# Low-half products one slab later, squares summed on TensorE and scalings on VectorE at the changes of sub-layer

## The chip, the core and the metric

The kernel runs on one core of one Trainium2 chip. The metric is the device time of one execution in microseconds, from the first to the last instruction with what lies around them; the lower the better. The core's engines work side by side, each through its own queue in order: PE (TensorE) multiplies matrices, with the weight loads shown apart as PEld; DVE (VectorE) and POOL (GpSimd) do elementwise work; ACT (ScalarE) copies, casts and applies functions; SP issues most DMAs. Semaphores join the queues.

## What is computed

A decoder trunk of two layers over 512 positions of width 1024. Each layer has four sub-layers: a half-step SwiGLU feed-forward (here "ffn1"), token mixing by three head groups with one output projection ("mix"), a second half-step feed-forward ("ffn2"), and a gated per-layer embedding ("ple"). Every sub-layer stands between two RMS norms and is added to the residual:

```python
for i in range(DEPTH):
    h = rmsnorm(x, g_ffn1_pre[i])
    x = x + 0.5 * rmsnorm(swiglu(h, w1_gate[i], w1_up[i], w1_down[i]), g_ffn1_post[i])
    h = rmsnorm(x, g_mix_pre[i])
    ...
    x = x + rmsnorm(mixed, g_mix_post[i])
    h = rmsnorm(x, g_ffn2_pre[i])
    x = x + 0.5 * rmsnorm(swiglu(h, w2_gate[i], w2_up[i], w2_down[i]), g_ffn2_post[i])
    h = rmsnorm(x, g_ple_pre[i])
    e = jax.nn.sigmoid(h @ w_ple_gate[i]) * (p[i].astype(x.dtype) @ w_ple_proj[i])
    x = x + rmsnorm(e, g_ple_post[i])
```

So between two sub-layers the program must finish the post-norm of the one, add to the residual x, and square, sum and scale x for the pre-norm of the next. This happens seven times (three times in a layer, and once between the layers); they are called **changes** below. After the last sub-layer there is only the post-norm and the output.

## The kernel before

x lies transposed in the core's memory: eight tiles (K slabs) of 128 features by 512 positions, in fp32. Every product is made of three matmuls in a rounded fp32 form: the weight and the input are each split into a high half and a low remainder (`wh`, `wl`, `xh`, `xl`), and the matmuls are wh·xh, wh·xl and wl·xh. They stand in `product` (lines 285, 286 and 287 in this order), so each weight tile of 128 columns takes 3 × 8 matmuls for the eight K slabs.

A change runs through two pieces of code, in two halves of 256 positions (`HALVES`, a and b).

`finish` (line 512) ends a sub-layer. It makes the last output tiles half by half; the outputs y are squared on ACT, and where a sub-layer makes more than two tiles in halves (mix: eight) the squares are added up ("folded", line 443) on POOL. Sums of squares over the features are matmuls of a square tile against a column of ones (`Rstd.add`, line 388; the tile `st`): a square tile is the loaded weight, and one column moves. In the program each is one matmul for 128 positions; in the profile each shows as two MATMUL rows. Nine small DVE steps turn `st` into the reciprocal root `rt` (line 368). PE transposes it (line 401, tile `rb`) and ACT copies the broadcast row out (`rbs`, line 402). Then `update` does the residual for each slab k: `scale` (line 570) multiplies y by the row, on DVE for even k and on POOL for odd k, and `add` (line 573) multiplies by the gain, a column, and adds x, on DVE.

`Entry` (line 449) begins the next sub-layer while `update` runs. For each slab ACT writes xh = x·gain (line 466), DVE writes xl = x·gain − xh (line 469), and ACT squares x; POOL folds the eight squares into one tile (line 443). The DVE queue in it is written by hand: update(k+1) stands ahead of xl(k). `products` (line 477) has PE's order by hand for half a: for each slab k, the three products of each of the `FIRST` = 3 first weight tiles; after slab `ROW_AT` = 5 it puts `row_b`, the transposes for half b of the row above. Then half b is updated, split and multiplied in the same way, with a fourth tile of whole width and, in ple, other work beside it. Behind the last of these products come the `st` matmuls over the squares of x, the nine small steps, and the row for the pre-norm, which the evacuations of the first tiles need.

All else (the order of most instructions within an engine's queue) is chosen by a scheduler when the program is built; SP's queue is the same before and after. In the four feed-forwards the gain is a column `half`, half of the post gain; the down-projection's outputs are copied from PSUM to y by DVE (lines 830 and 843), and the last tile's square is made from y (line 524).

Of the kernel before, what the change touches and what calls it, by code (L numbers as in the profile page):

```python
# [14 lines left out]
AF = mybir.ActivationFunctionType  # L15
ALU = mybir.AluOpType
# [6 lines left out]
NK = D // P  # L23
# [7 lines left out]
AT_DOWN = (3, 13)  # L31
# [4 lines left out]
FIRST = 3  # L36
ROW_AT = 5
MORE = 1
PROJ = 8
LAST_POOL = (2, 6)  # L40
DIRECT = 2
# [66 lines left out]
HALVES = (slice(0, S // 2), slice(S // 2, S))  # L108
# [49 lines left out]
def hybrid_trunk(ctx: ExitStack, tc: tile.TileContext, a: dict, out: bass.AP):  # L158
    nc = tc.nc
    V, A, T, G = nc.vector, nc.scalar, nc.tensor, nc.gpsimd  # L160
# [7 lines left out]
    def slot(dt=F32, name="s", tag="s"):  # L168
        return sp.tile([P, S], dt, tag=tag, name=name, bufs=SLOTS[tag])
# [35 lines left out]
    x = [cst.tile([P, S], F32, name=f"x{k}") for k in range(NK)]  # L205
# [26 lines left out]
    half = cst.tile([P, DEPTH, 2, 8], F32, name="half")  # L232
    for l in range(DEPTH):
        for i, n in enumerate(("ffn1_post", "ffn2_post")):
            V.tensor_scalar(out=half[:, l, i, :], in0=gains[:, l, G_COLS[n]:G_COLS[n] + 8],
                            scalar1=0.5, scalar2=None, op0=ALU.mult)
# [41 lines left out]
    def product(o, w, xs, first=True, cols=slice(0, S), tick=lambda: None, last=True):  # L278

        oc = o[:, cols]  # L280
        n = len(xs)
        for k in range(n):
            (wh, wl), (xh, xl) = w[k], xs[k]
            kw = dict(skip_group_check=True)
            T.matmul(oc, wh, xh[:, cols], start=first and k == 0, stop=False, **kw)  # L285
            T.matmul(oc, wh, xl[:, cols], start=False, stop=False, **kw)  # L286
            product.last = T.matmul(oc, wl, xh[:, cols], start=False, stop=last and k == n - 1, **kw)  # L287
            tick()
# [160 lines left out]
    class Entry:  # L449
# [3 lines left out]
        def __init__(self, l, name, update, row_b, tag):  # L453
            self.l, self.name, self.update, self.row_b = l, name, update, row_b
            self.xs = [(slot(F32R, "xh", tag), slot(F32R, "xl", tag)) for _ in range(NK)]
            self.tiles = [slot(name="sq") for _ in range(4)]
            self.sqs = [self.half(HALVES[0])]

        def half(self, c):
            sq = Squares(c, tiles=self.tiles)  # L460
            with tc.manual_schedule(engines={V.engine}):
                self.update(0, c)
                for k in range(NK):
                    g = gain(self.l, self.name, k)
                    h, lo = (t[:, c] for t in self.xs[k])
                    ia = A.activation(out=h, in_=x[k][:, c], func=AF.Copy, scale=g)
                    if k + 1 < NK:
                        self.update(k + 1, c)
                    iv = V.scalar_tensor_tensor(out=lo, in0=x[k][:, c], scalar=g, in1=f(h), op0=ALU.mult,  # L469
                                                op1=ALU.subtract)  # L470
                    sq.add(x[k][:, c])
            sq.fold()
            if c is HALVES[0]:
                self.tail = ia.ins, iv.ins
            return sq

        def products(self, tiles, more=lambda: None):


            ca, cb = HALVES  # L480
            with tc.manual_schedule(engines={T.engine}):
                for k in range(NK):
                    for w, o in tiles:
                        product(o, w[k:k + 1], self.xs[k:k + 1], k == 0, ca, last=k == NK - 1)
                    if k == ROW_AT:
                        self.row_b()
            self.sqs.append(self.half(cb))
            for w, o in tiles:
                product(o, w, self.xs, False, cb)
            more()  # L490
            self.eps = eps_col()
            r = Rstd(D, keep=self.eps)
            with tc.issue_after(product.last.ins):
                for sq, c in zip(self.sqs, HALVES):
                    r.add(*sq.parts(), cols=c, last=True)
            self.rt = r.col()
            self.r, self.behind = r, rsqrt_cols.last.ins

# [13 lines left out]
    def finish(ys, sq, last, compute, evac, gcol, nxt, at, xtag="s", eps=None):  # L512


        rb = slot(name="rbs")
        row_tag = "d" if nxt and nxt[1].startswith("ffn") else None
        direct = {m: slot(name="sq") for m in list(last)[-DIRECT:]}
        tiles = [slot(name="sq") for _ in range(3 if len(last) > DIRECT else 0)]

        def evacuate(m, c, o, sqh, parts):  # L520
            if m in direct:
                t = direct[m]
                evac(m, c, o)
                A.activation(out=t[:, c], in_=ys[m][:, c], func=AF.Square)
                parts.append(t)
            else:
                evac(m, c, o)
                sqh.add(ys[m][:, c])

        ca, cb = HALVES  # L530
        ra, rb_ = Rstd(D, ca, eps=eps), Rstd(D, cb, eps=eps)
        sqa, sqb = (Squares(c, tiles=tiles) for c in HALVES)
        pa, pb, steps = [], [], [0]
        sq.fold()
        for m in last:
            evacuate(m, ca, compute(m, ca), sqa, pa)
            if len(pa) == 1:
                sqa.fold()

        def tick():  # L540
            steps[0] += 1
            if steps[0] == at[0]:
                ra.add(*sq.parts(), *sqa.parts(), *pa, last=True)
                ra.col()
            elif steps[0] == at[1]:
                ra.row(rb[:, ca], None)
                rb_.add(*sq.parts())

        with tc.manual_schedule(engines={T.engine}):
            for m in last:  # L550
                o = compute(m, cb, tick)
                rb_.add(*pb[-1:])
                evacuate(m, cb, o, sqb, pb)
                if len(pb) == 1:
                    sqb.fold()
            assert steps[0] >= at[1]
            rb_.add(*sqb.parts())
        rb_.add(*pb[-1:], last=True)

        def row_b():  # L560
            rb_.row(rb[:, cb], row_tag)

        def update(k, c):
            scale(k, c)
            add(k, c)

        def scale(k, c):
            y = ys[k][:, c]
            e = G if k % 2 or nxt is None and k in LAST_POOL else V
            e.tensor_tensor(out=y, in0=y, in1=rb[:, c], op=ALU.mult)  # L570

        def add(k, c):
            V.scalar_tensor_tensor(out=x[k][:, c], in0=ys[k][:, c], scalar=gcol(k), in1=x[k][:, c],  # L573
                                   op0=ALU.mult, op1=ALU.add)
            if nxt is None:
                nc.sync.dma_start(out=out[:, k, c], in_=x[k][:, c])

        if nxt is None:
            with tc.manual_schedule(engines={V.engine}):
                order = [k for k in range(NK) if k % 2 == 0 and k not in LAST_POOL]  # L580
                order += [k for k in range(NK) if k not in order]
                for k in order:
                    scale(k, ca)
                todo = list(order)

                def between():
                    if todo:
                        add(todo.pop(0), ca)

                between()  # L590
                between()
                rb_.col(between)
                while todo:
                    between()
                row_b()
                for k in order:
                    update(k, cb)
            return None
        rb_.col()
        return Entry(*nxt, update, row_b, xtag)  # L600
# [119 lines left out]
    def ffn(l, idx, state, nxt, xtag="s", early=None):  # L720
# [85 lines left out]
        sq, ys = Squares(), {}  # L806
# [13 lines left out]
        for m in range(NK - LAST_DOWN):  # L820
            if early is not None and m == TRIG_AT:
                early()
            if m < TOGETHER:
                o = together[m]
            else:
                o = bank()
                product(o, down(m), hid)
            ys[m] = slot(name="y")
            sq.add(o)
            V.tensor_copy(out=ys[m], in_=o)  # L830
        last = range(NK - LAST_DOWN, NK)
        w = {m: down(m) for m in last}

# [6 lines left out]
            ys[m] = slot(name="y")  # L840

        def evac(m, c, o):
            V.tensor_copy(out=ys[m][:, c], in_=o[:, c])

        return finish(ys, sq, last, compute, evac, lambda k: half[:, l, idx, k:k + 1], nxt, AT_DOWN, eps=state.eps)

    def trig():

# [481 lines left out]
    state = start()  # L1330
    for l in range(DEPTH):
        state = ffn(l, 0, state, (l, "mix_pre"), xtag="m" if l else "s", early=None if l else trig)
        state = mixer(l, state, (l, "ffn2_pre"))
        state = ffn(l, 1, state, (l, "ple_pre"))
# [59 lines left out]
```

## Time and profile before

Three runs took 2153.1, 2151.86 and 2143.6 us; the median is 2151.86.

| | us |
|---|---|
| median of the runs | 2151.86 |
| profiled execution, its own time | 2149.54 |
| its span, first to last instruction | 2147.7 |
| POOL folds of squares (line 443), 165 of them, busy | 174.1 |
| POOL scalings (line 570), 68 of them, busy | 60.3 |

A row of the profile's timeline has the start in us, the duration, engine, line, operation and the tile written `<-` the tiles read; behind it in brackets stands how long the engine was idle before, and what released it. A row of windows gives, for a stretch of time, the busy time of each engine with the count of its instructions, the granted TensorE clock (PEclk, 1.00 is full speed), and the DMA share and rate. The seven changes lie at about 355, 612, 990, 1060, 1425, 1685 and 2055 us of the span.

### The profile page before, as it was taken

Reading aid. Unit: us, or ns where it says so; the run is one execution under the profiler, and the core shown is the slowest. Engines: PE = TensorE matmul, PEld = TensorE weight load, DVE = VectorE, ACT = ScalarE, POOL = GpSimd, SP = SyncE. Lnnn points to the kernel's source line nnn. Section 1 sums busy time; section 2 is a strip of 40 time slices with the busy share of each in tenths; the row PEclk is TensorE's granted clock in tenths of the full one; section 3 lists DMA queues with packets and bytes.
Section 4 is the critical chain, followed back from the end, with each engine's and each line's share of the span. In section 5 each row is a group of like instructions: output and inputs, shape, how many; then the busy total and the mean of one; then the engine's idle time right before and its main releaser. Section 6 shows DMA issues by size and latency. Waiting matters only on the chain.

```text
span 2147.7 us, 35941 instructions
## 1 busy us (share of the span) xinstructions
PE 2066.4 (96%) x13264; PEld 1879.5 (88%) x13264; DVE 1552.6 (72%) x2851; ACT 1117.2 (52%) x2296; POOL 507.4 (24%) x498
## 2 busy tenths in 40 slices
PE   7999999999999999999889999999999999999996
PEld 6999988887888999888779999888878889998886
DVE  7788754878879888625798886357788798885376
ACT  6556533555656555524565555235555565564243
POOL 3111012226432111003431110131264421100043
PEclk9999999999999999999999999999999999999998
DMA  7667232211233776332427762323111348653321
GB/s 218 171 175 180 86 109 72 88 62 47 59 80 107 187 179 152 99 96 82 123 84 189 175 169 86 103 67 99 53 52 54 81 133 191 181 136 97 98 74 65
DMA packets 139425, 244.73 MB, mean 114 GB/s; under 512 B 15600, under 2 KB 26096, under 8 KB 139248
## 3 DMA queue, kind: packets, MB, share of 16 engines
q1 hardware_dynamic: 117792, 204.00, 30.1%
q0 software_dynamic: 20736, 37.76, 11.0%
q8 instruction: 104, 1.70, 0.3%
q10 hardware_dynamic: 720, 0.67, 0.1%
q14 instruction: 73, 0.60, 0.1%
HBM read 240.27 MB, written 2.10 MB: 113 GB/s over the span
## 4 chain that ended last, share of the span: by engine, by line
PE 81%; DVE 13%; ACT 2%; issue 2%; DMA 1%; POOL 0%; SPq 0%; DVEq 0%; ACTq 0%; POOLq 0%
PE ps L286 9%; PE ps L285 9%; PE ps L287 9%; PE ux L686 6%; PE ux L685 6%; PE ux L684 6%; PE uy L686 3%; PE uy L685 3%; PE uy L684 3%; DVE x L573 2%; PE in L286 2%; PE in L287 2%; PE in L285 2%; DVE wl L270 2%; DVE xl L469 2%; PE uz L686 2%
## 5 line engine op out<-in xcount | busy, mean ns | idle before, releaser
L270 DVE TENSOR_TENSOR wl<-raw,wh 128x512 fp32r<-128x512 f32 (+2 forms) x893 | 603.9, 691 | 393.7 <-ACT wh L269 342.2
L269 ACT CAST wh<-raw 128x512 fp32r<-128x512 f32 (+1 forms) x934 | 548.6, 605 | 578.1 <-PE ps L286 269.4
L443 POOL TENSOR_TENSOR sq<-sq 128x256 f32<-128x256 f32 (+1 forms) x165 | 174.1, 1056 | 734.8 <-ACT sq L433 730.6
L286 PE MATMUL ps<-l,wh 128*128 128x512 f32 (+1 forms) x824 | 302.8, 367 | 0.2 <-DVE l L198 0.2
L287 PE MATMUL ps<-h,wl 128*128 128x512 f32 (+1 forms) x824 | 301.9, 367 | 0.0
L285 PE MATMUL ps<-h,wh 128*128 128x512 f32 (+1 forms) x824 | 300.5, 368 | 0.0
L668 POOL DMA_DIRECT2D raw<-in_w_gu x144 | 125.9, 912 | 676.6 <-DMA raw<-in_w_gu 227.5
L686 PE MATMUL ux<-fh,wl 128*128 128x256 f32 x864 | 244.5, 283 | 0.0
L685 PE MATMUL ux<-fl,wh 128*128 128x256 f32 x864 | 244.5, 283 | 0.0
L684 PE MATMUL ux<-fh,wh 128*128 128x256 f32 x864 | 244.4, 283 | 0.0
L286 PE MATMUL ps<-xl,wh 128*128 128x256 f32 (+1 forms) x536 | 182.0, 348 | 11.4 <-DVE xl L469 11.2
L285 PE MATMUL ps<-xh,wh 128*128 128x256 f32 (+1 forms) x536 | 173.1, 349 | 18.6 <-ACT wh L269 10.1
L287 PE MATMUL ps<-xh,wl 128*128 128x256 f32 (+1 forms) x536 | 181.0, 344 | 0.0
L286 PEld LDWEIGHTS ps<-l,wh 128*128 128x128 f32 x824 | 155.7, 189 | 25.6 <-DVE l L198 0.8
L287 PEld LDWEIGHTS ps<-h,wl 128*128 128x128 f32 x824 | 155.4, 189 | 25.1 <-DVE wl L270 0.4
L285 PEld LDWEIGHTS ps<-h,wh 128*128 128x128 f32 x824 | 155.6, 189 | 24.8
L684 PEld LDWEIGHTS ux<-fh,wh 128*128 128x128 f32 x864 | 165.8, 192 | 0.5
L685 PEld LDWEIGHTS ux<-fl,wh 128*128 128x128 f32 x864 | 165.8, 192 | 0.5
L686 PEld LDWEIGHTS ux<-fh,wl 128*128 128x128 f32 x864 | 165.8, 192 | 0.0
L285 PEld LDWEIGHTS ps<-xh,wh 128*128 128x128 f32 x536 | 104.6, 202 | 31.9 <-ACT wh L269 11.3
L286 PEld LDWEIGHTS ps<-xl,wh 128*128 128x128 f32 x536 | 108.0, 203 | 23.6 <-DVE xl L469 14.5
L287 PEld LDWEIGHTS ps<-xh,wl 128*128 128x128 f32 x536 | 108.4, 203 | 10.8 <-DVE wl L270 1.1
(335 smaller groups left out, 5100.3 us busy)
## 6 DMA issues: line engine op xcount, KB each, us to landing
raw<-in_w_gu SPq DMA_DIRECT2D x424, 256.0 KB, 3.9
raw<-in_w_down SPq DMA_DIRECT2D x160, 256.0 KB, 2.6
raw<-in_w_gu POOLq DMA_DIRECT2D x144, 256.0 KB, 5.0
raw<-in_win_f SPq DMA_DIRECT2D x60, 256.0 KB, 2.7
raw<-in_ple_gate SPq DMA_DIRECT2D x32, 256.0 KB, 2.7
raw<-in_wo_a SPq DMA_DIRECT2D x18, 256.0 KB, 2.7
raw<-in_w_down SPq DMA_DIRECT2D x32, 128.0 KB, 2.1
raw<-in_wo_b SPq DMA_DIRECT2D x12, 256.0 KB, 2.7
```

The lines of the kernel that those rows point to most:

```text
L269: A.copy(out=h, in_=raw)
L270: (G if on == "g" else V).tensor_tensor(out=lo, in0=raw, in1=f(h), op=ALU.subtract)
L285: T.matmul(oc, wh, xh[:, cols], start=first and k == 0, stop=False, **kw)
L286: T.matmul(oc, wh, xl[:, cols], start=False, stop=False, **kw)
L287: product.last = T.matmul(oc, wl, xh[:, cols], start=False, stop=last and k == n - 1, **kw)
L443: G.tensor_tensor(out=self.acc[:, c], in0=self.acc[:, c], in1=self.last[:, c], op=ALU.add)
L469: iv = V.scalar_tensor_tensor(out=lo, in0=x[k][:, c], scalar=g, in1=f(h), op0=ALU.mult, op1=ALU.subtract)
L573: V.scalar_tensor_tensor(out=x[k][:, c], in0=ys[k][:, c], scalar=gcol(k), in1=x[k][:, c], op0=ALU.mult, op1=ALU.add)
L668: G.dma_start(out=self.raw[n], in_=self.part(m), accum_op=ALU.add)
L684: T.matmul(o, wh, xh, start=first and k == 0, stop=False, **kw)
L685: T.matmul(o, wh, xl, start=False, stop=False, **kw)
L686: T.matmul(o, wl, xh, start=False, stop=k == 3, **kw)
```

## The change

Four edits, all in the code of the changes:

- `Entry` squares each slab into a tile of its own (eight instead of four rotating ones), and nothing is folded: `Rstd.add` gets all eight tiles, so PE makes 8 × 4 = 32 `st` matmuls in a change instead of 4.
- `products` has the wh·xl products of a slab one slab later (`LAG` = 1), behind the wh·xh and wl·xh of the next.
- `scale` runs on DVE for all slabs; POOL keeps its share only at the end of the program.
- In the feed-forwards DVE multiplies by the gain where it copied from PSUM, so `add` is a plain sum; the last tile's square is read from PSUM, since y is scaled by then.

```diff
         def __init__(self, l, name, update, row_b, tag):
...
-            self.tiles = [slot(name="sq") for _ in range(4)]
-            self.sqs = [self.half(HALVES[0])]
+            self.sqs = [slot(name="sq") for _ in range(NK)]
+            self.half(HALVES[0])
 
         def half(self, c):
-            sq = Squares(c, tiles=self.tiles)
...
-                    sq.add(x[k][:, c])
-            sq.fold()
+                    A.activation(out=self.sqs[k][:, c], in_=x[k][:, c], func=AF.Square)
...
             with tc.manual_schedule(engines={T.engine}):
-                for k in range(NK):
-                    for w, o in tiles:
-                        product(o, w[k:k + 1], self.xs[k:k + 1], k == 0, ca, last=k == NK - 1)
+
+                for k in range(NK + LAG):
+                    kw = dict(skip_group_check=True)
+                    if k < NK:
+                        for w, o in tiles:
+                            T.matmul(o[:, ca], w[k][0], self.xs[k][0][:, ca], start=k == 0, stop=False, **kw)
+                            T.matmul(o[:, ca], w[k][1], self.xs[k][0][:, ca], start=False, stop=False, **kw)
+                    if k >= LAG:
+                        j = k - LAG
+                        for w, o in tiles:
+                            T.matmul(o[:, ca], w[j][0], self.xs[j][1][:, ca], start=False, stop=j == NK - 1, **kw)
                     if k == ROW_AT:
                         self.row_b()
...
             with tc.issue_after(product.last.ins):
-                for sq, c in zip(self.sqs, HALVES):
-                    r.add(*sq.parts(), cols=c, last=True)
+                for c in HALVES:
+                    r.add(*self.sqs, cols=c, last=True)
...
-                A.activation(out=t[:, c], in_=ys[m][:, c], func=AF.Square)
+                A.activation(out=t[:, c], in_=ys[m][:, c] if gcol else evac.square, func=AF.Square)
...
-            e = G if k % 2 or nxt is None and k in LAST_POOL else V
+            e = G if nxt is None and (k % 2 or k in LAST_POOL) else V
             e.tensor_tensor(out=y, in0=y, in1=rb[:, c], op=ALU.mult)
...
-            V.scalar_tensor_tensor(out=x[k][:, c], in0=ys[k][:, c], scalar=gcol(k), in1=x[k][:, c],
-                                   op0=ALU.mult, op1=ALU.add)
+            if gcol:
+                V.scalar_tensor_tensor(out=x[k][:, c], in0=ys[k][:, c], scalar=gcol(k), in1=x[k][:, c],
+                                       op0=ALU.mult, op1=ALU.add)
+            else:
+                V.tensor_tensor(out=x[k][:, c], in0=ys[k][:, c], in1=x[k][:, c], op=ALU.add)
...
-            V.tensor_copy(out=ys[m], in_=o)
+            V.tensor_scalar(out=ys[m], in0=o, scalar1=half[:, l, idx, m:m + 1], scalar2=None, op0=ALU.mult)
```

The rows below show the queues at the first change (ffn1 to mix of layer 0). A row has the line, the operation, the tile written and the tiles read, and the shape; line numbers of the change are those of its own file, some lines further down.

DVE before, at the first slabs of half a: `y<-y,rbs` is the scaling, `x_..<-y,half,x_..` the sum (x_73 to x_80 are the eight slabs of x), `xl` the low half.

```order
L570 TENSOR_TENSOR y<-y,rbs 128x256
L573 SCALAR_TENSOR_TENSOR x_73<-y,half,x_73 128x256
L573 SCALAR_TENSOR_TENSOR x_74<-y,half,x_74 128x256
L469 SCALAR_TENSOR_TENSOR xl<-x_73,gains,xh 128x256
L570 TENSOR_TENSOR y<-y,rbs 128x256
L573 SCALAR_TENSOR_TENSOR x_75<-y,half,x_75 128x256
L469 SCALAR_TENSOR_TENSOR xl<-x_74,gains,xh 128x256
L843 COPY y<-ps 128x256
```

DVE with the change, at the same place:

```order
L576 TENSOR_TENSOR y<-y,rbs 128x256
L583 TENSOR_TENSOR x_73<-y,x_73 128x256
L576 TENSOR_TENSOR y<-y,rbs 128x256
L583 TENSOR_TENSOR x_74<-y,x_74 128x256
L469 SCALAR_TENSOR_TENSOR xl<-x_73,gains,xh 128x256
L576 TENSOR_TENSOR y<-y,rbs 128x256
L583 TENSOR_TENSOR x_75<-y,x_75 128x256
L469 SCALAR_TENSOR_TENSOR xl<-x_74,gains,xh 128x256
L852 TENSOR_SCALAR y<-ps,half 128x256
```

Each slab has its scaling in DVE's own queue now, three DVE instructions to a slab instead of two and a half.

PE before, at the first slab of half a (`in` are the three first tiles of the mixer's input projection):

```order
L285 MATMUL in<-xh,wh 128x256
L286 MATMUL in<-xl,wh 128x256
L287 MATMUL in<-xh,wl 128x256
L285 MATMUL in<-xh,wh 128x256
L286 MATMUL in<-xl,wh 128x256
```

PE with the change, from the second slab's high halves on (lines 485 and 486), with the first slab's low halves (line 490) behind them:

```order
L485 MATMUL in<-xh,wh 128x256
L486 MATMUL in<-xh,wl 128x256
L485 MATMUL in<-xh,wh 128x256
L486 MATMUL in<-xh,wl 128x256
L485 MATMUL in<-xh,wh 128x256
L486 MATMUL in<-xh,wl 128x256
L490 MATMUL in<-xl,wh 128x256 x3
```

The second matmul of a slab waited for xl; now six matmuls of the next slab stand ahead of the first that reads it.

PE before, behind the last product of half b, where the squares are summed and the mixer's next product `vt` begins:

```order
L285 MATMUL in<-xh,wh 128x512
L286 MATMUL in<-xl,wh 128x512
L287 MATMUL in<-xh,wl 128x512
L388 MATMUL st<-con,sq 128x1 x4
L1098 MATMUL vt<-wh,xh 128x288
```

PE with the change, at the same place:

```order
L286 MATMUL in<-xh,wh 128x512
L287 MATMUL in<-xl,wh 128x512
L288 MATMUL in<-xh,wl 128x512
L389 MATMUL st<-con,sq 128x1 x32
L1110 MATMUL vt<-wh,xl 128x288
```

The four `st` matmuls became 32 in one block. In five of the seven changes the 32 stand together so; in the two from ffn2 to ple, 26 stand together and six are spread over the products just ahead.

More of the change, by code (lines that the diff above doesn't have):

```diff
@@ L38 @@
 MORE = 1
+LAG = 1
 PROJ = 8
@@ L470, in half @@
                                                 op1=ALU.subtract)
-                    sq.add(x[k][:, c])
-            sq.fold()
+                    A.activation(out=self.sqs[k][:, c], in_=x[k][:, c], func=AF.Square)
             if c is HALVES[0]:
                 self.tail = ia.ins, iv.ins
-            return sq
         def products(self, tiles, more=lambda: None):
@@ L481, in products @@
             with tc.manual_schedule(engines={T.engine}):
-                for k in range(NK):
-                    for w, o in tiles:
-                        product(o, w[k:k + 1], self.xs[k:k + 1], k == 0, ca, last=k == NK - 1)
+                for k in range(NK + LAG):
[8 more added lines that the diff above has]
+                            T.matmul(o[:, ca], w[j][0], self.xs[j][1][:, ca], start=False, stop=j == NK - 1, **kw)
                     if k == ROW_AT:
                         self.row_b()
-            self.sqs.append(self.half(cb))
+            self.half(cb)
             for w, o in tiles:
@@ L842, in evac @@
         def evac(m, c, o):
-            V.tensor_copy(out=ys[m][:, c], in_=o[:, c])
-        return finish(ys, sq, last, compute, evac, lambda k: half[:, l, idx, k:k + 1], nxt, AT_DOWN, eps=state.eps)
+            V.tensor_scalar(out=ys[m][:, c], in0=o[:, c], scalar1=half[:, l, idx, m:m + 1], scalar2=None, op0=ALU.mult)
+            evac.square = o[:, c]
+        return finish(ys, sq, last, compute, evac, None, nxt, AT_DOWN, eps=state.eps)
     def trig():
```

## The prediction

> **What bounds the kernel.** I read the page first, then the seven changes as windows, then one change row by row.
>
> ```profile
> PE 2066.4 (96%) x13264; PEld 1879.5 (88%) x13264; DVE 1552.6 (72%) x2851; ACT 1117.2 (52%) x2296; POOL 507.4 (24%) x498
> PE 81%; DVE 13%; ACT 2%; issue 2%; DMA 1%; POOL 0%; SPq 0%; DVEq 0%; ACTq 0%; POOLq 0%
> ```
>
> PE is busy 96% of the span and makes 81% of the chain that ended last. So time is won only where PE stands idle or runs at a lower clock, and what is put into its queue costs its whole length. The changes of sub-layer are where PE waits:
>
> ```profile
> core 0: us, PE busy (x) PEld busy (x) DVE busy (x) ACT busy (x) POOL busy (x), PEclk, DMA share, GB/s
> 355.00:400.00 45.00, 39.10 (x292) 36.52 (x291) 37.36 (x82) 20.92 (x50) 22.37 (x24) 1.00 0.19 57
> 610.00:672.00 62.00, 58.04 (x383) 54.47 (x382) 50.99 (x103) 37.54 (x89) 32.17 (x36) 0.89 0.29 78
> 990.00:1045.00 55.00, 51.92 (x330) 46.82 (x330) 44.69 (x91) 31.34 (x66) 22.50 (x24) 0.97 0.29 96
> 1060.00:1104.00 44.00, 35.62 (x214) 33.56 (x213) 37.12 (x73) 25.87 (x65) 22.33 (x26) 0.81 0.19 43
> 1425.00:1466.00 41.00, 36.21 (x262) 34.08 (x261) 34.13 (x68) 19.51 (x47) 21.99 (x24) 0.96 0.14 43
> 1685.00:1736.00 51.00, 47.01 (x317) 44.44 (x316) 45.33 (x93) 33.22 (x80) 28.63 (x32) 0.90 0.20 57
> 2055.00:2096.00 41.00, 37.47 (x267) 34.41 (x267) 37.85 (x72) 24.07 (x54) 22.92 (x24) 1.00 0.24 80
> ```
>
> Length less PE busy gives the idle time: 5.9, 4.0, 3.1, 8.4, 4.8, 4.0 and 3.5 us, together 33.6. One less PEclk, times the length, gives what the lower clock took: 0, 6.8, 1.7, 8.4, 1.6, 5.1 and 0, together 23.6. So all there is to win in the changes is 57 us, 2.7% of the run. Part of it lies ahead of the first scaling, in stretches that the edits hardly touch:
>
> ```profile
> 610.00:632.50 22.50, 21.14 (x158) 20.26 (x157) 13.57 (x34) 9.19 (x21) 10.96 (x13) 0.92 0.47 108
> 1060.00:1071.20 11.20, 7.38 (x40) 7.02 (x39) 5.67 (x17) 4.07 (x10) 3.58 (x4) 0.70 0.59 120
> 1685.00:1700.90 15.90, 15.28 (x116) 15.00 (x115) 10.89 (x29) 7.85 (x19) 7.79 (x10) 0.89 0.31 75
> ```
>
> By the same sums these hold 3.2, 7.2 and 2.4 us. Some 44 us are in reach.
>
> **What the change wins: the waits for DVE.** In the first change PE waits for these (total us, number, longest), and its halves run so:
>
> ```profile
> PE in L286 <- DVE xl L469: 2.8, 5, 1.3
> PE rb L401 <- DVE rt L368: 2.2, 1, 2.2
> 366.10:382.50 16.40, 10.90 (x81) 9.65 (x79) 16.23 (x32) 7.92 (x20) 11.19 (x13) 1.00 0.10 28
> 382.50:397.40 14.90, 14.50 (x97) 13.17 (x98) 13.50 (x25) 8.52 (x23) 6.99 (x9) 1.00 0.16 44
> ```
>
> In half a (366.10 to 382.50) DVE is busy 16.23 of 16.40 us: it sets the pace, and PE's 10.90 fit inside. DVE is slow there because its instructions are long while POOL works:
>
> ```profile
> L570 POOL TENSOR_TENSOR y<-y,rbs x32: 836/918/981, 363.2 to 2081.3; 128x256 f32<-128x256 f32 x32
> L570 DVE TENSOR_TENSOR y<-y,rbs x32: 406/418/1505, 363.4 to 2088.1; 128x256 f32<-128x256 f32 x32
> ...
> 385.23 0.47 DVE L573 SCALAR_TENSOR_TENSOR x<-y,half,x 128x256 f32<-128x256 f32 x1
> 385.63 0.47 DVE L469 SCALAR_TENSOR_TENSOR xl<-x,gains,xh 128x256 fp32r<-128x256 f32 x1
> 386.03 0.41 DVE L570 TENSOR_TENSOR y<-y,rbs 128x256 f32<-128x256 f32 x1
> 386.47 0.85 DVE L573 SCALAR_TENSOR_TENSOR x<-y,half,x 128x256 f32<-128x256 f32 x1
> ```
>
> The same scaling takes DVE 0.41 us alone and up to 1.5 beside POOL. Undisturbed steps give the new price of a slab, start to start: scaling to sum 0.44, sum to low half 0.40, low half to next scaling 0.40, together 1.24 us. What else stands in DVE's queue there, and PE's pace:
>
> ```profile
> 369.57 0.41 DVE L843 COPY y<-ps 128x256 f32<-128x256 f32 x1
> ...
> 378.64 0.15 DVE L368 SCALAR_TENSOR_TENSOR r_w<-r_q 128x2 f32<-128x2 f32 x1
> 378.82 0.16 DVE L368 SCALAR_TENSOR_TENSOR rt<-r_w,r_z 128x2 f32<-128x2 f32 x1
> 378.90 1.29 DVE L270 TENSOR_TENSOR wl<-raw,wh 128x512 fp32r<-128x512 f32 x2
> ...
> 624.38 0.28 PE L286 MATMUL wo<-ml,wh 128*128 128x256 f32 x1
> 624.50 0.28 PE L287 MATMUL wo<-mh,wl 128*128 128x256 f32 x1
> ```
>
> PE starts a matmul of this width every 0.12 us, nine to a slab: 1.08. DVE still leads, by little. From the first scaling at 363.4: eight slabs at 1.24 (9.9 us), nine small steps at 0.18 (1.6), the copy (0.4) and, in case it still stands there, one weight remainder (0.6): the last low half ends near 376, and `rt` with it, 3 us before the 378.82 of now. The transposes stand behind slab 5 and wait for `rt` as before; they take 0.4 us, and the 21 matmuls behind them 2.5. Half a then ends near 378.9 instead of 382.5: 3.6 us won. The lag itself adds little to that: what follows the last low half are three matmuls instead of eight, 0.6 us, and the transposes cover it. Half b has only its 0.4 us of idle PE to win. Together 4.0 of the 5.9 us, 68%. The same share of the 44 in reach is **30 us won**; the ends are 17 (the wait for `rt`, whose steps stand late in DVE's order, takes back half of the first change's 4.0 and as much of the others) and 44 (all).
>
> The 56 scalings that move are 56 × 0.41 = 23 us more on DVE, inside this pace. The products from PSUM replace copies of the same shape (the 0.41 above), so I cost them at nothing; should one take the 0.47 of a sum, 64 of them would be 4 us, and PE waits for few of those. SP's queue is the same, and POOL's own DMAs stand behind fewer folds.
>
> **What it costs: the sums on PE.** 28 more `st` matmuls in each of seven changes, two rows each in the profile: 392 rows.
>
> ```profile
> 397.39 0.95 PE L388 MATMUL st<-con,sq 128*128 128x1 f32 x8
> 398.20 0.38 PE L1098 MATMUL vt<-wh,xh 128*128 128x288 f32 x1
> ...
> 625.39 1.50 PE L388 MATMUL st<-con,sq 128*128 128x1 f32 x12 [0.62 <-POOL sq L443]
> 626.76 0.43 PE L285 MATMUL wo<-mh,wh 128*128 128x256 f32 x1
> ...
> 638.91 2.55 PE L388 MATMUL st<-con,sq 128*128 128x1 f32 x12
> 641.33 0.56 PE L286 MATMUL ps<-xl,wh 128*128 128x256 f32 x1
> ```
>
> Start to next start, 8 rows take 0.81 us (0.10 each) and 12 take 1.37 (0.114 each): one moving column, but a whole weight load each, and no neighbour to hide it. In a block of 64 rows the longer one is nearer: 392 × 0.114 = **45 us**, 40 by the shorter. PE has other work at that point (`vt`, the next products), so nothing covers this.
>
> **And the clock.** The third pair above is 0.20 us a row: there the granted clock was half. Why it fell is in these windows, cut where the clock steps:
>
> ```profile
> 374.32:377.74 3.42, 2.24 (x17) 1.83 (x15) 3.39 (x9) 1.94 (x5) 2.86 (x4) 1.00 0.00 0
> 377.74:381.15 3.41, 2.12 (x18) 2.12 (x19) 3.34 (x8) 1.09 (x3) 1.76 (x3) 1.00 0.12 35
> 623.50:626.91 3.41, 2.79 (x24) 2.59 (x23) 1.75 (x3) 1.43 (x4) 2.48 (x3) 1.00 0.24 78
> 626.91:630.32 3.41, 3.41 (x17) 3.41 (x18) 2.30 (x10) 1.45 (x3) 1.04 (x2) 0.50 0.25 76
> 637.15:640.56 3.41, 3.41 (x18) 3.41 (x17) 3.06 (x7) 2.48 (x7) 1.95 (x3) 0.50 0.05 17
> ```
>
> PE busy for 2.24 of 3.42 us kept the full clock (first two rows). PE busy for 2.79 of 3.41 lost it (next two), and 1.4 us of that were the 12 `st` rows. In the fifth PE is busy throughout, half of it with `st`, and the clock stays low. So `st` rows seem to count as idle: only with them taken off do the rows fall in line. A block of 64 rows lasts 64 × 0.114 = 7.3 us, longer than two such stretches, so one whole stretch always holds nothing else, and the clock falls 2 to 5.6 us into the block, say 3.9. The remaining 30 rows then cost 0.20 instead of 0.114: 2.6 us. Behind the block the clock returns after a stretch full of work, some 4.4 us at half speed: 2.2 us. That is 4.8 a change where the 32 stand together, 3.8 in the two with 26: 5 × 4.8 + 2 × 3.8 = **32 us**. The ends are 0 (the clock holds) and 45 (6.4 a change).
>
> The Trainium skill, TensorE: Matmul & The Clock Gate, Part 1, says that the clock halves after an idle window of about 3.4 us; the window's length agrees with the rows above. By its practical rule, no idle gap over 3.4 us, a PE that keeps issuing would stay fast, and the sum would lack the 32 us. The row at 623.50, with 0.8 us without a PE instruction, speaks against that reading.
>
> **The sum.** 45 + 32 − 30 = +47 us on the profiled execution's own 2149.5 (its span is 2147.7; the median of the runs, 2151.9, lies 2.3 above it): about 2196.
>
> **The rivals.**
>
> *The clock holds.* Two windows of one kind are thin evidence. Then 45 − 30 = +15: 2164, and 2159 with the shorter price of a row. This is what the page's rule, read by gaps, would give here.
>
> *DVE or `rt` keeps the pace.* The transposes wait for `rt` as long as before, mix still folds its own output squares on POOL ahead of half a (the change doesn't do quite what it says there), and only 17 us are won: 45 + 32 − 17 = +60: 2210. For it speaks that `rt` stands almost last in DVE's queue; against it, that DVE's slab falls from 2 us (16.4 over eight) to 1.24.
>
> *The sums hide.* PEld is busy 88% of the span beside PE, so most weight loads do run under other matmuls. If those of the block ran under the products around it, the 392 rows would cost nothing, PE would count as working, the clock would hold, and the waits would decide: −30, 2120. It decides below 30 / 392 = 0.077 us a row. Against it: every block measured above is dearer, 0.10 and more.
>
> **Chances and range.** Forecast 0.63, clock holds 0.16, DVE keeps the pace 0.15, sums hide 0.06. The range leaves out the last case and the outermost bounds: from 2157, the clock holding with a little more won than forecast, to 2214, DVE's case with a little more lost to the clock. A measurement of this kernel can tell about 0.5%, 11 us, from no change. Faster by more than that: 0.06. Within: 0.08, the lower half of the case in which the clock holds. Slower: 0.86.
>
> **What would show it.** Right: `st` rows of 64 at 0.11 to 0.20 us just behind half b; PEclk near 0.5 in the stretch from there on, in all seven changes; no scaling or Entry fold on POOL in them; DVE sums and low halves at 0.41 to 0.47 us; half a of the first change some 3.6 us shorter, with a wait for `rt` left. Wrong: PEclk 1.00 behind the blocks (the first rival), half a as long as before (the second), `st` rows under 0.077 us (the third).

## The result, and the profile after

The changed kernel took 2203.43 us in the median of four runs (2202.78 to 2204.53), the kernel before 2148.56 (2143.6 to 2153.1): a ratio of 1.0257, 95% interval 1.0243 to 1.0272. It is slower by 55 us. The profiled execution took 2203.08, with a span of 2201.3 us against 2147.7.

The page of the changed kernel, busy time and chain:

```profile
PE 2132.9 (97%) x13656; PEld 1941.6 (88%) x13656; DVE 1512.5 (69%) x2907; ACT 1114.9 (51%) x2296; POOL 373.0 (17%) x344
PE 85%; DVE 9%; ACT 3%; issue 1%; DMA 1%; POOL 0%; SPq 0%; DVEq 0%; ACTq 0%; POOLq 0%
```

PE has the 392 rows more (13,656 against 13,264) and 66.5 us more of busy time. POOL lost 134 us (its folds went from 165 to 67, with none of `Entry`'s left, and its scalings from 68 to 12, all at the end of the program), and DVE, though it has 56 instructions more, lost 40; its share of the chain fell from 13% to 9%. What PE waits for over the whole run, before (first fence) and after (second); total us, number, longest:

```profile
PE rb L401 <- DVE rt L368: 11.9, 8, 3.9
PE ps L286 <- DVE xl L469: 11.2, 10, 2.1
...
PE in L286 <- DVE xl L469: 5.0, 8, 1.3
```

```profile
PE rb L402 <- DVE rt L369: 16.0, 9, 3.7
...
PE ps L485 <- ACT xh L466: 1.4, 4, 0.5
```

The 16.2 us of waits for `xl` are gone; 4 us of them came back as waits for `rt`. The seven blocks of sums, as windows of the changed kernel:

```profile
391.50:400.40 8.90, 8.90 (x67) 8.86 (x65) 0.48 (x2) 0.43 (x1) 0.00 (x0) 0.80 0.39 121
678.70:688.00 9.30, 9.30 (x67) 9.26 (x65) 4.15 (x7) 2.96 (x6) 0.00 (x0) 0.76 0.59 140
1042.60:1051.10 8.50, 8.50 (x54) 8.50 (x54) 1.90 (x3) 1.31 (x3) 0.00 (x0) 0.66 0.29 94
1121.60:1133.20 11.60, 11.60 (x66) 11.56 (x65) 4.36 (x8) 2.70 (x6) 0.29 (x1) 0.60 0.53 115
1486.70:1498.10 11.40, 11.40 (x65) 11.36 (x65) 0.46 (x1) 0.43 (x1) 0.00 (x0) 0.60 0.27 86
1774.20:1783.30 9.10, 9.10 (x66) 9.06 (x64) 4.20 (x7) 3.01 (x6) 0.86 (x1) 0.77 0.59 145
2138.20:2146.70 8.50, 8.50 (x55) 8.50 (x54) 1.90 (x3) 1.34 (x3) 0.00 (x0) 0.66 0.18 62
```

PE is busy throughout in each (second number against the first), and yet PEclk lies between 0.60 and 0.80: the clock falls inside every block. The first block, row by row, in the timeline of the changed kernel:

```profile
391.37 0.39 PE L288 MATMUL in<-xh,wl 128*128 128x512 f32 x1
391.61 8.92 PE L389 MATMUL st<-con,sq 128*128 128x1 f32 x64
400.39 0.59 PE L1110 MATMUL vt<-wh,xl 128*128 128x288 f32 x1
...
402.21 0.44 PE L1109 MATMUL vt<-wl,xh 128*128 128x288 f32 x1
...
404.57 0.29 PE L1108 MATMUL vt<-wh,xh 128*128 128x288 f32 x1
```

64 rows take 8.8 us (at 0.111 a row, the price at full clock, it would be 7.1), and the `vt` products behind them run at half speed, 0.24 us from start to start, until the clock is back at 403.6 and they take 0.13.

To see where the 54 us of span come from, I paired the matmuls of two traces, `st` rows left out, in order of start (13,008 in each), and took how much later the second kernel reaches the matmul of the same place in that order. Between the changes and the mixers nothing moves. Summed over the stretches (us, against the profiled run of before; "mixer" is what lies between the change into it and the change out of it):

| kernel | start | seven changes | mixer of layer 0 | mixer of layer 1 | end |
|---|---|---|---|---|---|
| changed | −3.5 | +40.6 | +10.1 | +6.5 | 0 |

The same pairing is used for every run below. Its start column differs by some 2 us from run to run, always below the one profiled run of before, whose clock fell longer there; nothing is read from it.

### The profile page after: what moved, and what is told of

Same layout as the page of the kernel before. It is cut to its first block, busy times and chain, and to the rows that moved or that the text cites. A ratio compares the mean times of both kernels' runs of the same rounds, so it can differ in the third digit from the quotient of the medians.

```text
span 2201.3 us, 36531 instructions
## 1 busy us (share of the span) xinstructions
PE 2132.9 (97%) x13656; PEld 1941.6 (88%) x13656; DVE 1512.5 (69%) x2907; ACT 1114.9 (51%) x2296; POOL 373.0 (17%) x344
## 4 chain that ended last, share of the span: by engine, by line
PE 85%; DVE 9%; ACT 3%; issue 1%; DMA 1%; POOL 0%; SPq 0%; DVEq 0%; ACTq 0%; POOLq 0%
PE ps L286 10%; PE ps L287 10%; PE ps L288 10%; PE ux L695 6%; PE ux L694 6%; PE ux L693 6%; PE st L389 4%; PE uy L695 3%; PE uy L694 3%; PE uy L693 3%; PE in L286 2%; PE in L288 2%; PE in L287 2%; PE uz L695 2%; PE uz L694 2%; PE uz L693 2%
## 5 line engine op out<-in xcount | busy, mean ns | idle before, releaser
L444 POOL TENSOR_TENSOR sq<-sq 128x512 f32<-128x512 f32 (+1 forms) x67 | 87.6, 1308 | 812.2 <-ACT sq L434 808.3
L286 PE MATMUL ps<-xh,wh 128*128 128x512 f32 (+1 forms) x416 | 134.7, 361 | 15.2 <-ACT wh L270 9.4
L288 PE MATMUL ps<-xh,wl 128*128 128x512 f32 (+1 forms) x416 | 145.5, 357 | 0.0
L287 PE MATMUL ps<-xl,wh 128*128 128x512 f32 (+1 forms) x416 | 143.7, 357 | 0.0
L389 PEld LDWEIGHTS st<-con,sq 128*128 128x128 f32 x648 | 97.7, 235 | 8.5 <-ACT sq L530 4.7
L286 PEld LDWEIGHTS ps<-xh,wh 128*128 128x128 f32 x416 | 77.7, 197 | 29.2 <-ACT wh L270 16.7
L389 PE MATMUL st<-con,sq 128*128 128x1 f32 x648 | 96.6, 277 | 5.8 <-ACT sq L530 3.8
```

Of the source, the lines that this page charges most:

```text
L389: T.matmul(self.st[:, i:i + 1], sq[:, b], ones_col, start=start, stop=last and n == len(sqs) - 1, skip_group_check=True)
L444: G.tensor_tensor(out=self.acc[:, c], in0=self.acc[:, c], in1=self.last[:, c], op=ALU.add)
```

## The experiments

**The parts one by one.** First the folds were put back into the changed kernel:

```diff
-                    A.activation(out=self.sqs[k][:, c], in_=x[k][:, c], func=AF.Square)
+                    sq.add(x[k][:, c])
+            sq.fold()
...
-                for c in HALVES:
-                    r.add(*self.sqs, cols=c, last=True)
+                for sq, c in zip(self.sqs, HALVES):
+                    r.add(*sq.parts(), cols=c, last=True)
```

> The changed kernel with POOL's folds of the entry squares put back (4 st matmuls a change), lag and DVE scalings kept. Theory A (the block of st rows costs the time): its 392 rows of 0.112 us (44 us), the extra time at half clock (22 us) and most of what the two mixers lost (16.6 us) go; the folds lengthen DVE's instructions again, so some of the 13 us or more won in the changes goes too: 2130 to 2150 us, no clock step behind the changes. Theory B (the loss comes from the scalings on DVE and the other order of the mixers, the rows being partly hidden): 2165 us or more, mixers still some 15 us longer than before.

It took 2155.43 us, ratio 1.0032 (1.0020 to 1.0045): 48 of the 55 us hang on the sums (less what the folds cost in their place). Theory B is out, but what is left is no gain either, and a little above Theory A's range.

The reverse, the kernel before with only that edit:

> The kernel before with only the 32 st matmuls a change in place of POOL's folds; scalings shared with POOL and no lag. Theory A: +44 us of rows, some +22 us of clock, up to +17 in the mixers, and about 10 us back because POOL's folds no longer lengthen DVE's instructions: 2195 to 2225 us. Theory B: the sums are the smaller part, 2160 to 2180 us.

2225.91 us, ratio 1.0347 (1.0322 to 1.0371), just above Theory A's range: the sums alone cost 77 us, 17 of them in the mixers, more than the whole change. In this kernel, where POOL still scales, `xl` takes 541 ns in the mean, against 491 with all edits. (A DVE sum of slabs takes 585 against 458, but with all edits it is a plain sum, another operation.)

Then the scalings alone, and the lag alone:

```diff
-            e = G if k % 2 or nxt is None and k in LAST_POOL else V
+            e = G if nxt is None and (k % 2 or k in LAST_POOL) else V
```

> The kernel before with only the scalings moved to DVE (and the gain multiplied in at the copy from PSUM); POOL still folds, no lag. Theory A: DVE loses POOL's 0.9 us scalings as a neighbour but takes 4 scalings of 0.41 us a half more; a small gain, 2133 to 2148 us. Theory B: DVE, which paces half a, becomes longer: 2155 to 2175 us.

> The kernel before with only the low-half products one slab later. Theory A (half a is paced by DVE, not by the order of PE): 2143 to 2150 us, no change. Rival (the waits of PE for xl, 2.8 us in the first change, go in all seven): 2125 to 2135 us.

The scalings (with the gain at the copies, as in the change): 2153.77 us, 1.0019 (1.0007 to 1.0032), between the two ranges. The lag: 2145.99 us, 0.9988 (0.9977 to 0.9999), next to nothing, as Theory A had it. By stretches:

| kernel | seven changes | mixer 0 | mixer 1 |
|---|---|---|---|
| folds back | −3.8 | +4.1 | +4.6 |
| sums only | +60.5 | +9.2 | +7.8 |
| scalings only | −11.1 | +4.6 | +6.6 |
| lag only | +1.2 | −1.0 | +1.1 |

(What follows the last change moved too, by +2.2 us with the folds back, +4.5 with the scalings only, and +4.3 with the scalings in five changes, a version shown below; that wasn't followed up.) So the scalings do win 11 us in the changes, and lose the same 11 in the mixers, of which the edit changes no line. What moved there is the order that the scheduler makes. Where the two mixers' matmuls are built in the order of before (lag only) nothing is lost; where some 500 matmuls of a mixer stand elsewhere, 4 to 10 us are. The timeline of the kernel before and of the changed one at the same place, a row and its transposes in the first mixer (the rows between are left out):

```profile
467.06 0.95 PE L388 MATMUL st<-con,sq 128*128 128x1 f32 x8
...
474.51 0.60 PE L401 MATMUL rb<-ident,rt 128*128 128x128 f32 x4
474.86 0.48 PE L287 MATMUL in<-xh,wl 128*128 128x512 f32 x1
```

```profile
476.77 1.05 PE L389 MATMUL st<-con,sq 128*128 128x1 f32 x8
...
484.19 0.44 PE L954 MATMUL z<-spl,conr 128*128 128x384 f32 x1 [1.28 <-DVE spl L190]
485.73 1.09 PE L402 MATMUL rb<-ident,rt 128*128 128x128 f32 x4 [1.09 <-DVE rt L369]
487.50 0.79 PE L286 MATMUL in<-xh,wh 128*128 128x512 f32 x1 [0.68 <-ACT rb L403]
```

Before, PE comes to the transposes with no wait; after, it waits three times, 3.1 us together, and the transposes run at half clock (a row takes 0.21 us from start to start instead of 0.11).

**What silence of POOL and the lag win, with nothing paid for it.** The changed kernel with `st` matmuls over the first square only:

```diff
-                    r.add(*self.sqs, cols=c, last=True)
+                    r.add(*self.sqs[:1], cols=c, last=True)
```

> The changed kernel with st matmuls over the first of the eight squares only, four a change as before the change: seven eighths of the sum of squares are left out, and neither POOL nor PE makes it. This is what silence of POOL and the lag win with nothing paid for it. The prediction's 30 us won would give 2120 us; Theory A by the phases of the changed trace (the changes win some 20 to 25 us, the mixers still lose up to 11 of them) gives 2132 to 2146 us. The second mixer's order is that of the kernel before here, the first one's is not: if the order is what the mixers lose by, the second loses nothing and the first some 4 us.

2109.82 us, ratio 0.9814 (0.9794 to 0.9834): better than either number. The seven changes win **39.8 us**; the first mixer, in the other order, loses 6.7, and the second, in the order of before, wins 1.5, as expected of the order. Two stretches of before (first fence) and the same work here (second), the changes into ffn2 and out of ple of layer 0:

```profile
600.00:712.00 112.00, 105.07 (x665) 95.79 (x665) 90.88 (x183) 64.32 (x143) 37.41 (x42) 0.92 0.40 107
1054.00:1134.00 80.00, 69.05 (x401) 62.37 (x400) 69.20 (x128) 47.08 (x104) 30.10 (x33) 0.89 0.35 95
```

```profile
600.50:703.18 102.68, 97.36 (x665) 88.73 (x665) 84.97 (x191) 63.86 (x143) 17.59 (x20) 1.00 0.44 118
1040.84:1110.26 69.42, 64.04 (x402) 57.33 (x401) 60.18 (x134) 45.34 (x101) 10.41 (x10) 0.98 0.40 105
```

They shrink by 9.3 and 10.6 us, and nearly all the clock that they lost (PEclk 0.92 and 0.89) is back. Shorter waits also leave the clock up.

**Why the clock falls in the blocks.** Three runs keep the 32 matmuls. In the first they are spread, one behind every third product of half b and of the next tile:

```diff
+            todo = [(k, c, b) for c in HALVES for k in range(NK) for b in range(2)]
+            product.after = lambda: todo and one(*todo.pop(0))
             for w, o in tiles:
                 product(o, w, self.xs, False, cb)
             more()
```

> The changed kernel with the same 32 st matmuls a change, but spread: each one behind three products of half b, or behind three of the next tile, where the scheduler can place it so. Theory A (a block of st rows counts as idle and halves the clock; the rows themselves keep their 0.11 us): the clock steps behind the changes go, the 44 us of rows stay: 2175 to 2190 us. Rival (spread between products the rows' weight loads run beside them): rows below 0.08 us and 2135 to 2165 us. Rival (the clock falls for another reason): 2198 to 2208 us, with the same steps.

2193.68 us, ratio 1.0205 (1.0186 to 1.0224): between Theory A and the last rival, so this run alone decides little. The scheduler spread about a third of the rows and left the others in groups, most of 10 to 18. The `st` rows alone in three windows of the first change, as the clock steps:

```profile
387.77:391.18 3.41, 1.37 (x13) 1.43 (x13) 0.00 (x0) 1.00 0.34 95
391.18:394.60 3.42, 2.88 (x26) 2.97 (x26) 0.00 (x0) 1.00 0.34 93
394.60:398.01 3.41, 2.49 (x12) 2.64 (x12) 0.00 (x0) 0.50 0.43 142
```

Where `st` took 1.37 of 3.41 us the clock stayed; where it took 2.88 it fell behind the window, though PE issued without a break. In the second and third run the blocks stay as they are, but the same sum is made in 64 or 8 equal columns:

```diff
-                    T.matmul(self.st[:, i:i + 1], sq[:, b], ones_col, start=start,
+                    T.matmul(self.st[:, i], sq[:, b], ones_wide, start=start,
```

> The changed kernel with 64 equal columns of ones in place of one in the 32 st matmuls of a change: the same 392 more rows in the same blocks, with 64 moving columns instead of one. Theory A (rows of one moving column count as idle): the blocks keep PEclk near 1.00 and the steps there go; a row takes as long as before or a little longer (0.11 to 0.14 us): 2175 to 2200 us. Rival (the clock falls because of the weight loads or of the waits, not of the single column): PEclk 0.6 to 0.8 in the blocks as now, 2203 us or more.

> The changed kernel with 8 equal columns of ones in the 32 st matmuls of a change, in place of one (2203 us) or 64 (2158 us); built in the same order as with 64. Theory A1 (what counts is the share of time in which columns move, and 8 of 64 is too little): the blocks still fall to a PEclk of 0.6 to 0.8, 2190 to 2203 us. Theory A2 (any width beyond one column is enough): 2155 to 2162 us.

With 64 columns 2157.68 us, ratio 1.0042 (1.0028 to 1.0056); with 8, 2202.32 us, 1.0240 (1.0206 to 1.0274). (The kernel with 8 is built in the order of the changed kernel, not in that of the one with 64, as the expectation had it; so it is compared with the changed kernel, and with the other one by the changes alone.) The first is below even Theory A's range, for two reasons that the stretches show: the wide blocks also leave fewer clock steps than the kernel before had, and the mixers, in yet another order, lost 12 us less. Windows of blocks, with 64 columns (first fence) and with 8 (second):

```profile
394.00:401.10 7.10, 7.10 (x66) 7.10 (x64) 0.46 (x1) 0.43 (x1) 0.00 (x0) 1.00 0.47 149
1108.70:1115.90 7.20, 7.20 (x67) 7.16 (x65) 4.14 (x7) 2.95 (x6) 0.17 (x1) 1.00 0.80 185
```

```profile
392.98:401.60 8.62, 8.62 (x65) 8.62 (x64) 0.46 (x1) 0.43 (x1) 0.00 (x0) 0.81 0.35 123
1122.90:1134.10 11.20, 11.20 (x65) 11.19 (x64) 4.32 (x8) 2.66 (x6) 0.43 (x1) 0.61 0.50 119
```

The number of rows, the weight loads and the place are the same; only how many columns move differs, and with it PEclk: 1.00 against 0.81 and 0.61. A row takes 0.111 us with 64 columns (7.1 us for 64), just what it takes with one at full clock. By stretches:

| kernel | seven changes | mixer 0 | mixer 1 |
|---|---|---|---|
| changed (1 column) | +40.6 | +10.1 | +6.5 |
| spread | +32.3 | +6.0 | +8.2 |
| 8 columns | +38.7 | +10.0 | +8.4 |
| 64 columns | +5.6 | +4.1 | +0.1 |
| no sums | −39.8 | +6.7 | −1.5 |

**Versions that use it.** The wide sums with the squares written in the rounded form that the products use, the kernel before with wide sums and nothing else, and the five changes that don't lead into a mixer with DVE scaling all slabs:

```diff
-            self.sqs = [slot(name="sq") for _ in range(NK)]
+            self.sqs = [slot(F32R, name="sq") for _ in range(NK)]
```

```diff
-            e = G if k % 2 or nxt is None and k in LAST_POOL else V
+            own = nxt is not None and nxt[1] != "mix_pre"
+            e = G if k % 2 and not own or nxt is None and k in LAST_POOL else V
```

> The changed kernel with 64 columns of ones in every st matmul, and the squares of x and the last output squares written in the rounded fp32 form that the products use, so that an st matmul over them should be one row instead of two. Theory (a row costs its 0.11 us of weight load, and the clock holds): against the 2157.7 us of the wide sums 32 rows a change go, 7 x 32 x 0.112 = 25 us: 2125 to 2140 us, faster than the kernel before. Rival (a matmul in the rounded form with so few columns takes as long as two rows): 2150 to 2160 us.

> The kernel before with 64 columns of ones in place of one in every st matmul, nothing else. Theory (one moving column counts as idle, so the 8 to 12 st rows that it has in the changes help to lower its clock): half of the 23.6 us that the lower clock takes in its changes goes, 2134 to 2142 us. Rival (blocks as short as these don't decide, only PE's waits do): 2146 to 2152 us.

> The kernel before with DVE scaling all slabs in the five changes that don't lead into a mixer, POOL's share kept in the other two; folds on POOL, no lag, no gain at the copies. The mixers' order is that of the kernel before. Theory (the scalings on DVE win some 6 us in those changes and lost it in the mixers by their order): 2139 to 2145 us, mixers unchanged. Rival (they cost DVE as much as they save): 2146 to 2152 us.

The first took 2139.02 us, 0.9948 (0.9933 to 0.9963): a matmul is one row now, 32 in a block, at 0.109 us; the changes win 21.8 us and the mixers, in another order, lose 14.8. The total is inside its theory's range, but the clock did not hold everywhere. The `st` rows alone in the stretch that one block of these rounded rows fills, in the stretch behind it, and in one that they fill in part:

```profile
1098.58:1101.99 3.41, 3.41 (x32) 3.41 (x31) 0.00 (x0) 1.00 1.02 193
1101.99:1105.40 3.41, 0.24 (x2) 0.10 (x1) 0.16 (x1) 0.50 0.56 187
1453.56:1456.98 3.42, 2.52 (x23) 2.41 (x22) 0.16 (x1) 1.00 0.32 108
```

In this kernel and in the last one below, three stretches of 3.41 us held 3.0 us or more of rounded rows with 64 columns, PE busy throughout, and behind each the clock fell; where such stretches held 2.8 us or less it stayed. The fp32 rows with 64 columns filled whole stretches (395.92 to 399.34, for one) and kept it. Why the two differ was not tried.

The second took 2139.66 us, 0.9950 (0.9933 to 0.9966), as its theory said, but not where it said: the clock steps in its changes got fewer, the changes as a whole moved by only −0.7, and 5.7 us were won in the mixers. That a faster PE wins nothing in the changes fits DVE setting the pace there, as in half a of the first, but wasn't tested apart. The third took 2145.01 us, 0.9986 (0.9972 to 0.9999): 5.9 us won in the changes, the mixers unharmed (−2.4), as forecast, at the upper end of the theory's range (4.3 us were lost behind the last change).

Last, all of it by change: the four edits with wide, rounded sums in the five changes that lead elsewhere, the code of before with wide sums in the two that lead into a mixer.

```diff
+            self.own = name != "mix_pre"
...
+                    if self.own:
+                        A.activation(out=self.sqs[k][:, c], in_=x[k][:, c], func=AF.Square)
+                    else:
+                        sq.add(x[k][:, c])
```

> A version put together from the parts: in the five changes that don't lead into a mixer the four edits with the rounded squares (one st row to a matmul), in the two that do the code of before (folds and half of the scalings on POOL, no lag), 64 columns of ones in every st matmul. Theory, from the phases of the last two kernels: the mixers keep their order and win 5.7 us, the five changes win 15.6, the start 2: 2122 to 2132 us, faster than both kernels and than the two last ones (2139). Rival (the gains overlap, the five changes' clock steps are the same ones that the wide columns alone removed): 2133 to 2140 us.

2121.47 us, ratio **0.9879 (0.9856 to 0.9901)**: 1.2% faster than before, half a microsecond below the expected range (the changes −16.9, the mixers −5.7). It beats both kernels.

## Why the prediction was right, point by point

It said 2196, and 2203.4 was measured. Three terms can be read from the stretches: no sums against before is what is won in the changes, 64 columns against no sums is what the rows cost, and 1 column against 64 is what the clock costs.

| term | predicted | in the seven changes |
|---|---|---|
| won | −30 (17 to 44) | −39.8 |
| rows of the sums | +45 | 5.6 + 39.8 = +45.4 |
| clock | +32 (0 to 45) | 40.6 − 5.6 = +35.0 |
| mixers | 0 | +16.6 |

- **The rows.** 0.114 us a row, 0.111 measured. The nearer of the two blocks gave the price, and nothing hid it. At 0.111 us 392 rows are 43.5 us; the other 2 of the +45.4 were not traced, so the agreement to half a microsecond is partly luck.
- **The clock.** That `st` rows count as idle was read from two windows; 64 columns against 8 and 1 show it for fp32 rows. In the first block the clock fell 5.2 us in (391.6 to 396.8), and in the seven blocks 2.2 to 5.2 us in, inside the forecast's 2 to 5.6. In and behind them it stayed at half for 75 us, which is 37.5 us lost, near the +35.0 that the stretches give. The rival in which it holds is out for one column, and is what happens with 64.
- **No gap, and yet the clock falls.** The block at 391.61 has no gap at all between its rows, and the clock fell in it, to a PEclk of 0.80 over the whole window. The Trainium skill, TensorE: Matmul & The Clock Gate, Part 1, asks for no PE-idle gaps over some 3.4 us. Here that is not enough, and the trace decides: a stretch of instructions that move few columns acts as the gap does. (The prediction set 0.8 us without a PE instruction at 623.50 against that rule; by its own row, 2.79 busy of 3.41, it was 0.6.)
- **Half a of the first change.** This is the window from the first product of half a to the first of half b in the changed kernel, and in it the stretch in which PE waits for `rt`:

```profile
362.76:376.77 14.01, 11.52 (x82) 11.13 (x81) 13.41 (x42) 9.05 (x23) 0.00 (x0) 0.88 0.13 33
369.48:372.90 3.42, 0.93 (x9) 0.73 (x8) 3.28 (x12) 2.43 (x7) 0.00 (x0) 1.00 0.00 0
```

  14.0 us instead of 16.4: 2.4 won, not 3.6. DVE's part was right: `rt` ended 12.3 us behind the first scaling (359.89 to 372.20), forecast 12.6. What wasn't forecast is the price of the wait: PE stood for 2.5 of 3.4 us, and the next 3.4 ran at half clock (PEclk 0.88 over the half).
- **DVE beside POOL.** The steps of a slab in DVE's timeline of the changed kernel:

```profile
364.51 0.42 DVE L576 TENSOR_TENSOR y<-y,rbs 128x256 f32<-128x256 f32 x1
364.96 0.42 DVE L583 TENSOR_TENSOR x<-y,x 128x256 f32<-128x256 f32 x1
365.31 0.48 DVE L469 SCALAR_TENSOR_TENSOR xl<-x,gains,xh 128x256 fp32r<-128x256 f32 x1
365.70 0.42 DVE L576 TENSOR_TENSOR y<-y,rbs 128x256 f32<-128x256 f32 x1
```

  1.19 us from scaling to scaling, forecast 1.24, with POOL still; before, single ones took up to 1.5. The Trainium skill, SBUF — State Buffer, SBUF: two separate sides, says that a VectorE operation with two SBUF inputs and a GpSimd operation that reads SBUF lock each other out for a whole instruction. The traces agree so far as they go: from 0.64 us before, the sums alone bring the mean of `xl` to 0.54 us, the scalings alone leave it at 0.66, and both bring it to 0.49.
- **The win as a whole was too small by 10 us.** The step that failed is "the same share of the 44 in reach", 68% by the first change. That share counted idle time and lost clock alike. In the changes into ffn2 and out of ple the clock came back nearly whole once the waits were short, and those two won 9.3 and 10.6 us in layer 0, half of the 39.8. (The prediction's lower end, 17, doesn't follow from its own words either: half of its share is 15 us, by which the rival built on it gives 2212 instead of 2210.)
- **The mixers were left out.** The step that failed is the silent one that edits in the changes cost only there. The scheduler built both mixers in another order, and they lost 16.6 us. That order and loss go together is shown: of the kernels above, those with the order of before or nearly so, with another matmul in at most 63 of a mixer's 1,004 places (lag, no scalings into the mixer, wide sums on the kernel before, the last version, and the second mixer alone with 64 columns and with no sums) are between −3.6 and +1.1, all others, with another one in 454 to 531 places, between +4.1 and +10.1. In the kernel without the sums both mixers have the same edits ahead of them, and only the one in another order loses. Why the scheduler changes its mind was not tried.

So the 7 us between forecast and measurement are the rest of larger errors: 10 too little won, 3 too little for the clock, 17 of the mixers missed, and 3 of the start by chance. That they nearly cancel is luck. The rivals: DVE does set the pace in the change, but wins more than the forecast gave; the sums that hide would need rows under 0.077 us, and in no block did they come below 0.10.

## What to carry to other kernels

Count what a helper engine's work costs on the engine that sets the end: silence of POOL and the lag won 40 us in the changes, the matmuls that took over the folds cost 80, nearly half of it through the clock. A reduction against a column of ones got cheaper here by moving 64 equal columns, which kept the clock in fp32, and by having its input in the rounded form, which halves the rows; blocks in the rounded form still lost the clock where they took 3.0 us or more of a stretch of 3.4. And where a scheduler orders the program, measure an edit by stretches: gains of 11 us in the changes were lost again in the mixers, which no edit touched, and were kept once the edits were left out of the two changes that lead there.

## What the runs showed of the hardware

- A block of 64 (or 52) fp32 matmul rows with whole weight loads and 1 or 8 moving columns lets the granted clock fall inside it, with PE issuing throughout; with 64 columns it stays at 1.00 in all seven. That is 35 us in seven blocks. Where between 8 and 64 the line lies was not tried.
- A row takes 0.111 us with 1, 8 or 64 columns at full clock; 64 columns cost nothing more.
- An fp32 `st` matmul shows as two rows, one whose inputs are in the rounded form as one (0.109 us): 32 rows instead of 64 in a block. Three stretches of 3.41 us with 3.0 us or more of such rows, of 64 columns, lost the clock all the same.
- One wait of PE of 2.5 us in a stretch of 3.4 was enough to halve the clock for the next 3.4.
